# An empty scheduling step moved from the end of a tile to its middle, in two generators of a hybrid-encoder kernel

## The chip, the cores and the metric

The kernel runs on one core of one Trainium2 chip. The metric is the device time of one execution in microseconds (us). The engines are TensorE (PE; its weight loads are listed as PEld), VectorE (DVE), ScalarE (ACT), GpSimd (POOL), and SyncE (SP), whose queue issues the transfers. Each engine works through its own list of instructions in order, and the engines wait for each other by semaphores.

## The reference: what is computed

One encoder layer is applied to 1280 rows, of which 1024 are one request and 256 another, each row 2048 wide. The rows are normalised and multiplied by one wide weight matrix. Its columns feed three mixers, whose outputs are gated, joined and multiplied by an output matrix.

```python
hn = rms_norm(x, norm_g)
proj = hn @ w_in
xbc, z_ssd, dt_raw, q, k, v, z_att, mq, z_mem = split_cols(proj, IN_SIZES)
...
y_f = ssd_scan(xs, dt[:, :, 0], A[0], Bm, Cm)
y_b = ssd_scan(xs[:, ::-1], dt[:, ::-1, 1], A[1], Bm[:, ::-1], Cm[:, ::-1])[:, ::-1]
...
o_att = window_attention(q, k, v, sink) * jax.nn.silu(z_att)
...
sm = jnp.einsum('bthd,bmhd->bhtm', mq, mk).astype(jnp.float32) * (MEM_HEAD_DIM ** -0.5)
pm = jax.nn.softmax(sm, axis=-1).astype(mv.dtype)
o_mem = jnp.einsum('bhtm,bmhd->bthd', pm, mv).reshape(b, T, MEM_WIDTH) * jax.nn.silu(z_mem)

return x + jnp.concatenate([o_ssd, o_att, o_mem], axis=-1) @ w_out
```

The scan runs in chunks of 128 rows. From each chunk come a state product (B transposed times the weighted inputs) for either direction and a product inside the chunk, the diagonal part. Memory attention has four heads of 128 over 256 memory rows.

## The kernel before, in words

The rows are ten tiles of 128, eight of the long request (0 to 7) and two of the short one (8 and 9). The weight matrices go by in blocks of columns. Each block is a loop over the depth of the product: a weight tile is loaded (`wraw`, four buffers), ACT rounds it to its high part (`wh`, line 206), DVE takes the rest (`wl`, line 207; three buffers each), and PE multiplies both parts with the rows' two parts into PSUM tiles called `acc` (lines 258 to 260 and 293 to 295). A step of that loop is 15 matmuls of 512 columns (288 in the block `kv`) or 24 of 320 columns.

The mixers run beside these blocks. Each is a Python generator per tile: `attn`, `mem_attn`, `ssd_up` (the ascending pass of the scan), `ssd_down` and some preparations. Two queues of generators, the lanes, take turns. After each step of a block, `pump` adds the lane's rate to a credit and runs one generator step for each whole credit: the code up to the next `yield`. A step that has nothing between two `yield`s is empty: it uses up a credit and leaves time to what was issued before it. A generator that reaches its end is taken off its lane in that step, and the next one starts with the next credit. So the place of a piece of work in a generator sets beside which block matmuls it lands; a scheduler then orders the instructions of neighbouring steps a little further, with the work of the weight split ahead of the rest.

In memory attention a tile goes through these pieces: `scores(0)` and `scores(1)` (two heads each: products `pms`, maxima, exponentials and division into `mpr`), `turn_(0)` and `turn_(1)` (PE transposes, `pmt<-identr,mprw` at line 631; ACT copies them to `mpT`, line 819), `values(0)` and `values(1)` (PE products `pmo<-mpT,mv`, line 830, multiplied with the gate by DVE into `moT`) and the store. `fetch_next` loads the next tile's input ahead.

In `ssd_up` a tile begins with transposes `pxs` and the products `pcb`. Then for each of two head groups g come a product with the state (`pyf`, line 934), the weighted inputs for both directions, rounded by ACT (`fh`, line 931, and `bh`) with the rests by DVE (`fl`, `bl`), and two state products `pst` of three matmuls each (lines 917 to 919). At the end `diag` does the products inside the chunk, `py`, which ACT copies to `yo` and SP stores to `yd`.

All products beside the blocks share three PSUM tiles, the pool `mix`. Such a product waits until the tile it gets has been emptied by DVE or ACT.

Of the kernel before, what the change touches and what calls it, by code (L numbers as in the profile page):

```python
# [44 lines left out]
def hymba_encoder_kernel(  # L45
# [37 lines left out]
    def psum(name):  # L83
        return mix.tile([P, 512], F32, tag="mix", name=name)
# [37 lines left out]
    def rsqrt(dst, src, scale, n):  # L122
        G.tensor_scalar(out=dst, in0=src, scalar1=scale, scalar2=EPS, op0=ALU.mult, op1=ALU.add)
        G.tensor_tensor(out=dst, in0=dst, in1=mhalf[:, :n], op=ALU.pow)

    def hv(ap, n=8):
        return ap.rearrange("p (h d) -> p h d", h=n)

    def hb(ap, n, d):
        return ap.unsqueeze(2).broadcast_to([P, n, d])  # L130
# [287 lines left out]
    def w2(name):  # L418
        return mp.tile([P, 512], F32, tag="wa", name=name, bufs=WA)
# [86 lines left out]
    def taken(name, t):  # L506
        return fetched.pop((name, t)) if (name, t) in fetched else fetch[name](t)

    def fetch_next():

        name = lanes[0][1][0] if len(lanes[0]) > 1 else ("", 0)
        if name[0] in fetch:
            fetched[name] = fetch[name[0]](name[1])
# [109 lines left out]
    def slot(i, name, shape, dtype=F32):  # L623

        return mp.tile([P] + shape, dtype, tag=f"lg{i}", name=name, bufs=1)
# [3 lines left out]
    def turn_words(out, words, wrote):  # L629

        i = T.transpose(out.bitcast(F32R), words, identr)  # L631
        for w in wrote:
            tc.add_manual_dep(i.ins, w.ins.name, WRITTEN, reason="the words' writer")

    def as_words(i, name, shape):

        w = slot(i, name, shape, F32R)
        G.memset(w.bitcast(F32)[(slice(None),) + tuple(slice(n - 1, n) for n in shape)], 0.0)  # L638
        return w
# [115 lines left out]
    def mem_attn(t):  # L755
        grp, ti = divmod(t, 5)
        tc_ = slice(ti * P, (ti + 1) * P)
        qr = taken("mem_attn", t)
        q = qr.bitcast(F32)
        yield  # L760

        def turned():
            ps = psum("pmq")
            for h in range(4):
                T.transpose(ps[:, h * P:(h + 1) * P].bitcast(F32R), qr[:, h * P:(h + 1) * P], identr)
            return ps

        tok_ = turned() if grp == 0 else q
        sq = w2("sq")
        A.activation(sq, tok_, AF.Square)  # L770
        ss = sm.tile([P, 4], F32, tag="s4", name="mss", bufs=4)
        V.reduce_sum(out=ss, in_=hv(sq, 4), axis=AX.X)
        r = sm.tile([P, 4], F32, tag="s4", name="mr", bufs=4)
        rsqrt(r, ss, 1.0 / P, 4)
        yield
        feat_ = q if grp == 0 else turned()
        qh = mp.tile([P, 512], F32R, tag="qT", name="mqh", bufs=2)
        A.activation(qh, feat_, AF.Copy)
        ql = mp.tile([P, 512], F32R, tag="qT", name="mql", bufs=2)
        V.tensor_sub(ql, feat_, qh.bitcast(F32))  # L780
        z = w2("zm")
        S.dma_start(hv(z, 4), zT_d[1][grp][:, :, tc_])
        yield
        yield
        st_ = {}

        def scores(hp):
            ps = psum("pms")
            for j in range(2):
                h = 2 * hp + j  # L790
                c = slice(h * P, (h + 1) * P)
                o = ps[:, j * 256:(j + 1) * 256]
                T.matmul(o, qh[:, c], mkH[:, h, :], start=True, stop=False)
                T.matmul(o, qh[:, c], mkL[:, h, :], start=False, stop=False)
                T.matmul(o, ql[:, c], mkH[:, h, :], start=False, stop=True)
            m = sm.tile([P, 2], F32, tag="m2", name="mm", bufs=10)
            V.reduce_max(out=m, in_=hv(ps, 2), axis=AX.X)
            V.scalar_tensor_tensor(out=m, in0=m, scalar=-1.0, in1=r[:, 2 * hp:2 * hp + 2], op0=ALU.mult, op1=ALU.mult)
            pr = slot(hp, "mpr", [512])
            den = sm.tile([P, 2], F32, tag="m2", name="mden", bufs=10)  # L800
            for j in range(2):
                A.activation(pr[:, j * 256:(j + 1) * 256], ps[:, j * 256:(j + 1) * 256], AF.Exp,
                             scale=r[:, 2 * hp + j:2 * hp + j + 1], bias=m[:, j:j + 1], accum_out=den[:, j:j + 1])
            V.reciprocal(out=den, in_=den)
            wrote = []
            for j in range(2):
                c = slice(j * 256, (j + 1) * 256)
                wrote.append(V.tensor_scalar(out=pr[:, c], in0=pr[:, c], scalar1=den[:, j:j + 1], scalar2=0.5,
                                             op0=ALU.mult, op1=ALU.mult))
            st_[hp] = wrote  # L810

        def turn_(hp):
            wrote = st_[hp]
            pr = as_words(hp, "mprw", [513])
            pt = psum("pmt")
            for a in range(4):
                turn_words(pt[:, a * P:(a + 1) * P], pr[:, a * P:(a + 1) * P], wrote[a // 2:a // 2 + 1])
            pT = slot(hp, "mpT", [512])
            A.activation(pT, pt, AF.Copy)
            st_[hp] = pT  # L820

        oT = w2("moT")

        def values(hp):
            pT = st_.pop(hp)
            po = psum("pmo")
            for j in range(2):
                h = 2 * hp + j
                for a in range(2):
                    T.matmul(po[:, j * P:(j + 1) * P], mv[:, a, h * P:(h + 1) * P],  # L830
                             pT[:, (2 * j + a) * P:(2 * j + a + 1) * P], start=(a == 0), stop=(a == 1))
            c = slice(hp * 256, (hp + 1) * 256)
            V.tensor_mul(oT[:, c], po[:, :256], z[:, c])

        scores(0)
        yield
        scores(1)
        yield
        yield
        yield  # L840
        turn_(0)
        yield
        turn_(1)
        yield
        values(0)
        fetch_next()
        yield
        values(1)
        S.dma_start(oT_d[1][grp][:, :, tc_], hv(oT, 4))
        yield  # L850


    def wb(name, dtype=F32, shape=(P, 512)):
        return mp.tile(list(shape), dtype, tag="wb", name=name, bufs=WBB)

    def ssd_up(t):
# [65 lines left out]
        for g in range(2):  # L922
            c = slice(g * 512, (g + 1) * 512)
            a = mp.tile([P, 512], F32, tag=f"ya{g}", name="ya", bufs=1)
            ya.append(a)
            rows(g)
            if not last:
                xf = wb("xf")
                V.tensor_mul(hv(xf), hv(xsT[g]), hb(dd_all[:, (t + 1) % 6, 8 * g:8 * g + 8], 8, 64))
                fh = wb("fh", F32R)  # L930
                A.activation(fh, xf, AF.Copy)
            if not first:
                pf = psum("pyf")
                T.matmul(pf, bc[:, 2 + g, :], state[:, c], start=True, stop=True)
                V.tensor_mul(hv(a), hv(pf), hb(eacs_all[:, t, 8 * g:8 * g + 8], 8, 64))
            yield
            if not last:
                fl = wb("fl", F32R)
                V.tensor_sub(fl, xf, fh.bitcast(F32))
            if not first:  # L940
                xb = wb("xb")
                V.tensor_mul(hv(xb), hv(xsT[g]), hb(dd_all[:, (t + 1) % 6, 16 + 8 * g:24 + 8 * g], 8, 64))
                bh = wb("bh", F32R)
                A.activation(bh, xb, AF.Copy)
            yield
            if not last:
                ps = psum("pst")
                into(ps, g, fh, fl)
                if t == 0 and g == 0:

                    need(mk_prep, range(4))
                if first:
                    V.tensor_copy(state[:, c], ps)
                else:
                    V.tensor_mul(hv(state[:, c]), hv(state[:, c]), hb(cd_all[:, t, 8 * g:8 * g + 8], 8, 64))
                    V.tensor_add(state[:, c], state[:, c], ps)
                yield
            if not first:
                bl = wb("bl", F32R)
                V.tensor_sub(bl, xb, bh.bitcast(F32))  # L960
                yield
                ps = psum("pst")
                into(ps, g, bh, bl)
                st = wb("st")
                A.activation(st, ps, AF.Copy)
                S.dma_start(sb_d[t][:, c], st)
                yield
# [69 lines left out]
        yield  # L1037
        yield
        diag()
        yield  # L1040


    last_y = {}
# [740 lines left out]
```

## Time and profile before

| what | value |
|---|---|
| median of 3 runs | 1775.0 us (1774.94 to 1775.37) |
| the profiled execution's own time | 1773.26 us |
| its span, first to last instruction | 1771.5 us |
| PE busy | 1762.3 us (99%) |
| weight loads of PE busy | 1608.5 us (91%) |
| DVE, ACT, POOL busy | 1245.5, 918.9, 550.5 us |
| bytes moved by the transfers | 301.16 MB |
| granted TensorE clock, mean | 1.000 |

The profiled execution is 1.74 us below the median of the runs, and its span is 1.76 us shorter than its own time. Busy time of PE counts a matmul from its start to a modelled end, and matmuls overlap, so a row's length is more than the distance to the next start. How long PE stood still is therefore read from the starts of two rows that follow each other, compared with the distance of the same two kinds of instruction elsewhere.

### The profile page before, as it was taken

The numbers are of one execution on the slowest core, as the hardware profiler recorded it, in microseconds if no ns is written. First come the engines' busy times: TensorE is split into PE (matmuls) and PEld (weight loads), VectorE is DVE, ScalarE is ACT, GpSimd is POOL, SyncE is SP. The second block draws the span as 40 slices with busy tenths as digits, with TensorE's granted clock in tenths as the row PEclk, the third lists the DMA queues.
The fourth block names the chain that finished last, engine by engine and source line by source line (L and its number), as shares of the span: only waits on it lengthen the run. The fifth ranks groups of instructions, "written<-read, shape, count | busy, mean of one in ns | idle before, by whom it ended". The sixth has DMA issues, their size and how long they took to land. (4 is left out here: it accounts for less than half of the span.)

```text
span 1771.5 us, 32002 instructions
## 1 busy us (share of the span) xinstructions
PE 1762.3 (99%) x11046; PEld 1608.5 (91%) x11046; DVE 1245.5 (70%) x2348; ACT 918.9 (52%) x2049; POOL 550.5 (31%) x980
## 2 busy tenths in 40 slices
PE   9999999999999999999999999999999999999999
PEld 7889999999998999999889988888988888899999
DVE  5596788888858878778765676557777654766665
ACT  5555455555434766766464565544446633543332
POOL 0105789998810101011001000011110000058775
PEclk9999999999999999999999999999999999999999
DMA  8554444445347644454635654557777864644442
GB/s 301 193 184 122 140 151 146 145 141 170 121 138 214 185 145 138 143 162 115 188 120 179 196 154 155 170 164 252 223 245 232 255 189 147 219 142 149 144 144 77
DMA packets 208211, 301.16 MB, mean 170 GB/s; under 512 B 19569, under 2 KB 86193, under 8 KB 208049
## 3 DMA queue, kind: packets, MB, share of 16 engines
q1 hardware_dynamic: 207904, 299.06, 54.5%
q8 instruction: 87, 1.43, 0.3%
q14 instruction: 76, 0.61, 0.1%
q10 hardware_dynamic: 144, 0.06, 0.0%
HBM read 236.36 MB, written 62.69 MB: 169 GB/s over the span
## 5 line engine op out<-in xcount | busy, mean ns | idle before, releaser
L207 DVE TENSOR_TENSOR wl<-wraw,wh 128x512 fp32r<-128x512 f32 (+1 forms) x480 | 346.5, 724 | 236.9 <-ACT wh L206 226.2
L206 ACT ACTIVATE wh<-wraw 128x512 fp32r<-128x512 f32 (+1 forms) x480 | 292.2, 613 | 296.4 <-PE acc L260 153.3
L258 PE MATMUL acc<-wh,xH 128*128 128x512 f32 (+1 forms) x1088 | 418.2, 385 | 0.5 <-DVE v_all L337 0.4
L260 PE MATMUL acc<-wh,xL 128*128 128x512 f32 (+1 forms) x1088 | 410.2, 377 | 0.0
L259 PE MATMUL acc<-wl,xH 128*128 128x512 f32 (+1 forms) x1088 | 409.9, 377 | 0.0
L258 PEld LDWEIGHTS acc<-wh,xH 128*128 128x128 f32 x1088 | 204.2, 188 | 37.1 <-issue 2.7
L260 PEld LDWEIGHTS acc<-wh,xL 128*128 128x128 f32 x1088 | 204.2, 188 | 36.7 <-issue 0.2
L259 PEld LDWEIGHTS acc<-wl,xH 128*128 128x128 f32 x1088 | 204.4, 188 | 35.5 <-issue 1.2
L293 PE MATMUL acc<-xH,wh 128*128 128x320 f32 x640 | 202.9, 317 | 0.0
L206 ACT ACTIVATE sh<-ws 128x384 fp32r<-128x384 f32 x176 | 91.3, 523 | 208.3 <-POOL ws L1259 109.8
L294 PE MATMUL acc<-xL,wh 128*128 128x320 f32 x640 | 198.7, 310 | 0.0
L295 PE MATMUL acc<-xH,wl 128*128 128x320 f32 x640 | 198.4, 310 | 0.0
L207 DVE TENSOR_TENSOR sl<-ws,sh 128x384 fp32r<-128x384 f32 x176 | 124.4, 710 | 97.7 <-ACT sh L206 97.3
L1259 POOL TENSOR_TENSOR ws<-wraw 128x128 f32<-128x128 f32 x176 | 112.3, 638 | 208.2 <-DMA wraw<-in_w_in_pairs_dram 82.8
L293 PEld LDWEIGHTS acc<-xH,wh 128*128 128x128 f32 x640 | 120.1, 188 | 2.7 <-issue 2.1
L294 PEld LDWEIGHTS acc<-xL,wh 128*128 128x128 f32 x640 | 120.2, 188 | 1.5 <-issue 1.2
L295 PEld LDWEIGHTS acc<-xH,wl 128*128 128x128 f32 x640 | 120.2, 188 | 0.8 <-issue 0.7
L1259 POOL TENSOR_TENSOR ws<-wraw,ws 128x128 f32<-128x128 f32 x176 | 115.2, 654 | 13.8
L1259 POOL TENSOR_TENSOR wraw<-wraw 128x128 f32<-128x128 f32 x176 | 112.4, 639 | 13.7
L1259 POOL TENSOR_TENSOR ws<-ws,wraw 128x128 f32<-128x128 f32 x176 | 116.1, 659 | 0.0
L638 POOL MEMSET lgw<- 128x1 f32 x40 | 3.9, 99 | 311.3 <-DVE lg L701 187.3
L362 DVE SCALAR_TENSOR_TENSOR c<-u,vec,c 128x638 f32<-128x638 f32 (+1 forms) x96 | 90.1, 939 | 2.2 <-ACT c L357 1.6
(440 smaller groups left out, 3951.0 us busy)
## 6 DMA issues: line engine op xcount, KB each, us to landing
wraw<-in_w_in_laid_dram SPq DMA_DIRECT2D x176, 256.0 KB, 3.0
wraw<-in_w_in_pairs_dram SPq DMA_DIRECT2D x112, 256.0 KB, 2.7
wraw<-in_w_out_laid_dram SPq DMA_DIRECT2D x64, 256.0 KB, 3.5
wraw<-in_w_out_pairs_dram SPq DMA_DIRECT2D x64, 256.0 KB, 2.7
rf<-ac SPq DMA_DIRECT2D x40, 256.0 KB, 4.1
rb<-ac SPq DMA_DIRECT2D x40, 256.0 KB, 5.0
wraw<-in_w_mem_laid_dram SPq DMA_DIRECT2D x32, 256.0 KB, 4.2
xst<-in_x_sample_dram SPq DMA_DIRECT2D x20, 256.0 KB, 5.3
```

The lines of the kernel that those rows point to most:

```text
L206: a = A.activation(h, raw, AF.Copy)
L207: b = V.tensor_sub(l, raw, h.bitcast(F32))
L258: T.matmul(ps[t][:, :n], sh, h[:, :n], start=(k_ == 0), stop=False)
L259: T.matmul(ps[t][:, :n], sh, l[:, :n], start=False, stop=False)
L260: T.matmul(ps[t][:, :n], sl, h[:, :n], start=False, stop=(k_ == KT - 1))
L293: T.matmul(o, sh, cur["H", q][:, m, c], start=(k == 0), stop=False)
L294: T.matmul(o, sh, cur["L", q][:, m, c], start=False, stop=False)
L295: T.matmul(o, sl, cur["H", q][:, m, c], start=False, stop=(k == KT - 1))
L362: V.scalar_tensor_tensor(out=c[0], in0=u[:, k:k + n], scalar=cw[k], in1=c[0], op0=ALU.mult, op1=ALU.add)
L638: G.memset(w.bitcast(F32)[(slice(None),) + tuple(slice(n - 1, n) for n in shape)], 0.0)
L1259: G.tensor_tensor(out=o, in0=x, in1=y, op=op)
```

## The change

`mem_attn` has its fourth empty step ahead of `turn_(0)` instead of after `values(1)`. `fetch_next` stands one piece earlier in the code, in the same step counted from the tile's start as before. `ssd_up` has one more empty step ahead of the first state product of group 0, and none after `diag`. The number of steps per tile stays as it is in both, and so does everything that is computed.

```diff
         scores(0)
         yield
         scores(1)
-        yield
-        yield
-        yield
+        for _ in range(4):
+            yield
         turn_(0)
         yield
         turn_(1)
+        fetch_next()
         yield
         values(0)
-        fetch_next()
         yield
         values(1)
         S.dma_start(oT_d[1][grp][:, :, tc_], hv(oT, 4))
-        yield
...
                 bh = wb("bh", F32R)
                 A.activation(bh, xb, AF.Copy)
             yield
+            if g == 0:
+                yield
             if not last:
                 ps = psum("pst")
                 into(ps, g, fh, fl)
...
         yield
         yield
         diag()
-        yield
```

On PE, memory attention of tile 1 falls into the second pass of the block `kv` (288 columns). Before, the second turn stands five block matmuls and more behind the first, in two halves:

```order
L631 MATMUL pmt<-identr,mprw 128x128 x4
L258 MATMUL acc<-wh,xH_7440 128x288
L259 MATMUL acc<-wl,xH_7440 128x288
L260 MATMUL acc<-wh,xL_7441 128x288
L258 MATMUL acc<-wh,xH_7440 128x288
L631 MATMUL pmt<-identr,mprw 128x128 x2
L259 MATMUL acc<-wl,xH_7440 128x288
L631 MATMUL pmt<-identr,mprw 128x128 x2
```

In the changed kernel the second turn follows a whole step of 15 block matmuls later:

```order
L631 MATMUL pmt<-identr,mprw 128x128 x4
L258 MATMUL acc<-wh,xH_7428 128x288
L259 MATMUL acc<-wl,xH_7428 128x288
...
L260 MATMUL acc<-wh,xL_7429 128x288
L631 MATMUL pmt<-identr,mprw 128x128 x4
L258 MATMUL acc<-wh,xH_7428 128x288
```

The first turn keeps its place there, and the second moves behind eleven more block matmuls and comes in one piece.

On PE again, at a block's end in `ssd_up` of tile 1, before (`po` is the value product of window attention, `ppt` its transposes):

```order
L631 MATMUL ppt<-identr,lgw 128x128 x4
L934 MATMUL pyf<-state,bc 128x512
L293 MATMUL acc<-xH_6806,wh 128x320
L726 MATMUL po<-pT,v_all 64x128 x16
L917 MATMUL pst<-fh,bth 128x512
```

and in the changed kernel, where the lines of `ssd_up` are two lower (915 to 917, 932):

```order
L631 MATMUL ppt<-identr,lgw 128x128 x4
L915 MATMUL pst<-bh,bth 128x512
L916 MATMUL pst<-bl,bth 128x512
L917 MATMUL pst<-bh,btl 128x512
L932 MATMUL pyf<-state,bc 128x512
L726 MATMUL po<-pT,v_all 64x128 x16
L915 MATMUL pst<-fh,bth 128x512
```

The three matmuls of a state product of group 0 have come down by two steps of 24 block matmuls and stand between the transposes and the products that need them.

On ACT, memory attention of tile 8, in the output blocks, before:

```order
L206 ACTIVATE wh<-wraw 128x512
L819 ACTIVATE mpT<-pmt 128x512 x2
L206 ACTIVATE wh<-wraw 128x512
L770 ACTIVATE sq<-mq 128x512
L206 ACTIVATE wh<-wraw 128x512
```

and in the changed kernel:

```order
L206 ACTIVATE wh<-wraw 128x512 x2
L819 ACTIVATE mpT<-pmt 128x512
L206 ACTIVATE wh<-wraw 128x512
L819 ACTIVATE mpT<-pmt 128x512
L770 ACTIVATE sq<-mq 128x512
L206 ACTIVATE wh<-wraw 128x512 x2
```

A weight split now stands between the copies of the two turns. On PE at that place the second turn, before together with the first, comes a step later, straight ahead of both value products:

```order
L260 MATMUL acc<-wh,xL_16351 128x512
L631 MATMUL pmt<-identr,mprw 128x128 x4
L830 MATMUL pmo<-mpT,mv 128x128 x8
L258 MATMUL acc<-wh,xH_16350 128x512
```

No block matmul is left between them; before, a step of 15 stood there.

## The prediction

> **What bounds the kernel now.** I read the page first, then the waits of PE for the stretch in which the moved pieces run, then PE's timeline at each place that the two orders show moved. The page:
>
> ```profile
> span 1771.5 us, 32002 instructions
> PE 1762.3 (99%) x11046; PEld 1608.5 (91%) x11046; DVE 1245.5 (70%) x2348; ACT 918.9 (52%) x2049; POOL 550.5 (31%) x980
> PEclk9999999999999999999999999999999999999999
> ```
>
> PE is the bound from end to end, at full clock. Neither kernel has a matmul more or less than the other, so only PE's standstills can change the time. The waits of PE between 540 and 1480 us (who waited, for whom, total, times, longest):
>
> ```profile
> PE pst L917 <- ACT fh L931: 0.9, 1, 0.9
> PE pmt L631 <- DVE mpr L808: 0.6, 1, 0.6
> PE pr L631 <- ACT so L1063: 0.5, 1, 0.5
> PE pmo L830 <- ACT mpT L819: 0.2, 1, 0.2
> ```
>
> That is 2.2 us, and three of the four belong to moved pieces. Modelled ends swallow part of a standstill, so I go by starts: what is lost is the distance of two starts beyond what the first instruction needs elsewhere.
>
> A page of the Trainium skill speaks against so small a stake: Perfetto Trace Analysis, section Identifying the Most-Contended Engine, calls matmul busy time a poor measure of PE's distance from its limit and sends the reader to the busy share of the weight loads. By that rule 9% of the span would be open to gain.
>
> ```profile
> L258 PEld LDWEIGHTS acc<-wh,xH 128*128 128x128 f32 x1088 | 204.2, 188 | 37.1 <-issue 2.7 <-ACT kraw L334 0.6 <-ACT xH L200 0.5
> ```
>
> This row answers it: the loader idles 37.1 us on this line, almost all without a releaser, since a load takes 188 ns and a matmul of 512 columns starts every 0.23 us (1332.82 to 1333.05 below). I keep the rule as a rival with a small chance.
>
> **The change part by part.** A step moved by one place lands one step of the block later: 15 starts of 0.23 us, 3.4 us, in the blocks of 512 columns, and 15 of 0.13 us in `kv`. Of memory attention's 80 transposes 36 change their place among the block matmuls and of its 80 value products 48; the rest stay, because the scheduler sorts inside a step or because two steps fall behind the same block matmuls.
>
> *Second turn of memory tile 1, in `kv`.*
>
> ```profile
> 846.97 0.29 PE L260 MATMUL acc<-wh,xL 128*128 128x288 f32 x1
> 847.10 0.29 PE L258 MATMUL acc<-wh,xH 128*128 128x288 f32 x1
> 848.00 0.33 PE L631 MATMUL pmt<-identr,mprw 128*128 128x128 f32 x2 [0.60 <-DVE mpr L808]
> 848.17 0.38 PE L259 MATMUL acc<-wl,xH 128*128 128x288 f32 x1
> 848.38 0.29 PE L631 MATMUL pmt<-identr,mprw 128*128 128x128 f32 x2
> ```
>
> ```profile
> 847.50 0.62 DVE L808 TENSOR_SCALAR mpr<-mpr,mden 128x256 f32<-128x256 f32 x2
> ```
>
> A block matmul takes 0.13 us (846.97 to 847.10), so the turn was due at 847.23 and came at 848.00: 0.77 us lost, and 0.08 at the second half (848.17 to 848.38 is 0.21). DVE's division ends at 848.12. Eleven block matmuls later the turn is due about 1.4 us later than now: the wait goes. Gain **0.85**.
>
> *Value products of memory tiles 2 and 4, a state product of scan tile 1.*
>
> ```profile
> 849.90 1.05 PE L830 MATMUL pmo<-mpT,mv 128*128 128x128 f32 x8
> 850.71 0.38 PE L258 MATMUL acc<-wh,xH 128*128 128x288 f32 x1
> ```
>
> ```profile
> 876.81 1.06 PE L830 MATMUL pmo<-mpT,mv 128*128 128x128 f32 x8
> 878.10 1.16 PE L830 MATMUL pmo<-mpT,mv 128*128 128x128 f32 x8 [0.24 <-ACT mpT L819]
> ```
>
> ```profile
> 933.25 0.31 PE L294 MATMUL acc<-xL,wh 128*128 128x320 f32 x1
> 933.40 0.31 PE L295 MATMUL acc<-xH,wl 128*128 128x320 f32 x1
> 933.80 1.05 PE L830 MATMUL pmo<-mpT,mv 128*128 128x128 f32 x7
> ```
>
> ```profile
> 656.70 0.71 PE L293 MATMUL acc<-xH,wh 128*128 128x320 f32 x1
> 657.34 1.10 PE L726 MATMUL po<-pT,v_all 128*64 128x128 f32 x16
> ```
>
> A half of the values (x8) takes 0.81 us undisturbed. In tile 2 the next half starts 1.29 us on: 0.48 lost. The changed order puts the first half behind three block matmuls and the second behind twelve more: gain **0.48**. In tile 4 a start of 0.15 became 0.40; one more block matmul stands ahead: gain **0.15**. At 656.70 a 0.15 us start became 0.64 because `po` waits for its transposes' copies; the state product that now stands between (three starts of 0.23, less one block matmul of 0.15) covers the 0.49: gain **0.49**.
>
> *Second turn of memory tile 7.*
>
> ```profile
> 1387.77 0.46 PE L631 MATMUL pmt<-identr,mprw 128*128 128x128 f32 x4
> 1388.07 0.50 PE L910 MATMUL pxs<-identr,xc 128*128 128x128 f32 x4
> 1388.40 0.46 PE L258 MATMUL acc<-wh,xH 128*128 128x512 f32 x1
> 1388.82 0.54 PE L631 MATMUL pmt<-identr,mprw 128*128 128x128 f32 x4
> ```
>
> A start of 0.42 where 0.23 is due; fourteen block matmuls later it is gone: gain **0.19**.
>
> *First state product of scan tile 8,* the largest wait of the view and the one the extra step stands ahead of.
>
> ```profile
> 1332.82 0.39 PE L260 MATMUL acc<-wh,xL 128*128 128x512 f32 x1
> 1333.05 0.80 PE L631 MATMUL pmt<-identr,mprw 128*128 128x128 f32 x8
> 1334.72 0.50 PE L917 MATMUL pst<-fh,bth 128*128 128x512 f32 x1 [0.88 <-ACT fh L931]
> ```
>
> ```profile
> 1332.88 1.26 ACT L974 ACTIVATE rf<-rf,wj_all 128x128 f32<-128x128 f32 x4
> 1334.06 0.61 ACT L931 ACTIVATE fh<-xf 128x512 fp32r<-128x512 f32 x1
> ```
>
> Eight turns (0.30 for four, 1387.77 to 1388.07) end near 1333.65, so over 1.0 us is lost. The order shows the product only two block matmuls further, with four transposes gone from ahead of it, and ACT still has the four `rf` ahead of `fh`, which ends at 1334.67 as now. Two times 0.23 less 0.30: gain **0.1**; the rest, 0.9, stays.
>
> Gains: 0.85 + 0.48 + 0.15 + 0.49 + 0.19 + 0.1 = 2.3 us; at the least none, at the most 3.2 with the remaining 0.9.
>
> *New waits.* In memory tile 8 the second turn now stands ahead of both value products, with a weight split between the two copies on ACT.
>
> ```profile
> 1431.13 0.49 PE L830 MATMUL pmo<-mpT,mv 128*128 128x128 f32 x3
> ```
>
> ```profile
> 1431.38 0.63 ACT L206 ACTIVATE wh<-wraw 128x512 fp32r<-128x512 f32 x1 [2.53 <-issue]
> ```
>
> ```profile
> 848.76 0.60 ACT L819 ACTIVATE mpT<-pmt 128x512 f32<-128x512 f32 x1 [0.18 <-PE pmt L631]
> ```
>
> From the block's end, 1431.13, PE reaches the second value product after 0.30 + 0.81 = 1.1 us. ACT starts the split 0.25 us in, takes 0.63, then 0.60 for the copy: 1.5 us. Cost **0.4**; none if the copy finds ACT free, 1.0 if a second split gets ahead.
>
> Four places pile up products that share the three `mix` tiles: about 738 us (turns, `pyf`, scores of window attention, no block matmul between), 787 and 1382 us (`py` beside scores), 1389 us (`pxs` round a turn, then `pyf`). Their waits for emptying are not in the trace; the nearest row is one emptying by DVE that starts too late:
>
> ```profile
> 1389.45 0.69 DVE L912 COPY xs<-pxs 128x512 f32<-128x512 f32 x1
> ```
>
> So 0 to 0.7 each; since one or two other products cover most of each, I take 0.25: **1.0**. In sum new waits cost 1.4, between 0 and 3.8.
>
> *The transfers and POOL.* `fetch_next` keeps its step. The stores of `moT`, `sb`, `yp`, `yd` and the loads of `rf` and `rb` move with their steps past weight loads on SP, 1168 transfers in both. In the last scan tiles `diag` is now in the step just before `ssd_down` begins, which loads `yd` back. SP's waits between 1425 and 1470 us:
>
> ```profile
> SPq L213 <- DVE wl L207: 11.4, 6, 2.8
> ```
>
> Weight loads wait for a free buffer, up to four splits ahead of use; a store that holds the queue takes from that wait. The reader of `yd` is nine steps away. I cost both at nothing; without that cover, a late weight tile costs PE what it is late. On POOL one pair of small instructions swaps.
>
> Sum: -2.3 + 1.4 = -0.9. The profiled execution would go from 1773.26 to 1772.4; the runs' median lies 1.74 us above it, so **1774.1 us**.
>
> **The rivals.** *The piled products eat the gain*: new waits near their upper end, 3.8 - 2.3 = +1.5, 1776.5. For it: three `mix` tiles serve both lanes. Against: most moved pieces keep block matmuls between them.
>
> *ACT's queue turns against PE, slower.* A copy `mpT` at ACT's head waits for a turn that now comes a step later, with a weight split queued behind it; if the split is late by the 3.4 us step, PE stands for it. In the view of `pmt`:
>
> ```profile
> who waited for it (us, times):
>   ACT wh L206: 7.6, 3
> ```
>
> Splits have waited so already, without PE waiting for a split in that stretch, since they run ahead; that speaks against it. It decides from two full steps lost in the 20 copies: 2 x 3.4 - 2.3 = +4.5, 1779.5.
>
> *More was hidden than I count.* All of 3.2 goes without new waits, and standstills inside modelled matmuls, the weight loads' idle time among them, go too: from 0.4 more on it is faster by over 0.2%; 1771.2 or less. Against it: outside these places starts are even. The skill's rule stands behind this case.
>
> *The scheduler undoes the shift*: 1775.0. The orders speak against it.
>
> **How the numbers follow.** My forecast (net -2.3 to 0) has 0.62, piled products 0.17, ACT's queue 0.10, hidden gain 0.10, no shift 0.01. A difference of 0.2%, 3.55 us, is about what a measurement of this kernel tells from none: under 1771.45 is faster, over 1778.55 slower. So faster 0.10, same 0.62 + 0.17 + 0.01 = 0.80, slower 0.10. The costs' bounds give 1775.0 - 3.2 = 1771.8 and 1775.0 + 3.8 = 1778.8; eight in ten lie within 1771.6 to 1777.2.
>
> **What would show it.** Right: no wait of `pmt` for `mpr` in `kv`; even starts at `po` near 657 and `pmo` near 878; the wait of `pst` for `fh` near 1334 still there; a new wait of about 0.4 of `pmo` for `mpT` near 1432. Wrong: waits of PE for `wl` or `wh` between 820 and 1480, new ones at `pcb`, `pyf` or `psc` of more than 0.7, or PE starts in the blocks that have become closer.

## The result, and the profile after

The changed kernel takes 1777.04 us (median of 22 runs) and the kernel before 1774.97 us (22 runs beside them): a ratio of 1.0012, 95% interval 1.0007 to 1.0018. That is 2.1 us more, inside the 0.2% that counts as no change here, but clearly not less. The forecast was 0.9 us less. The profiled execution took 1775.66 us with a span of 1774.0 us, 2.4 us more than the one of before. In 15 of the 22 runs the mean granted clock was 1.000 and their median is 1776.47 us, while the runs of the kernel before at 1.000 in the three series of runs below have medians of 1773.89 to 1774.49 us, so the loss does not come from a lower clock.

The page after, its span and PE's row:

```profile
span 1774.0 us, 31995 instructions
PE 1763.1 (99%) x11046; PEld 1608.5 (91%) x11046; DVE 1247.0 (70%) x2348; ACT 920.5 (52%) x2049; POOL 552.9 (31%) x980
```

PE has the same 11046 matmuls. The waits of PE between 540 and 1480 us in the changed kernel (who waited, for whom, total, times, longest):

```profile
PE psc L692 <- DVE nm L694: 1.2, 1, 1.2
PE pxs L908 <- DMA xc<-xbc_d: 0.9, 2, 0.7
PE pst L915 <- ACT fh L929: 0.7, 1, 0.7
PE pr L631 <- ACT so L1062: 0.5, 1, 0.5
PE pk L539 <- DVE kh L533: 0.4, 1, 0.4
PE pxs L908 <- ACT mpr L802: 0.2, 1, 0.2
```

The two waits of memory attention (`pmt` for `mpr` 0.6, `pmo` for `mpT` 0.2) are gone. Three new ones stand in their place: scores of window attention (`psc`) for the maxima that DVE takes, the scan's input transposes (`pxs`) for their load, and the transposes of k (`pk`) for their rounding. The prediction had a wait of more than 0.7 us at `psc` among its signs of being wrong, and that sign came; but none of its terms has a price for any of the three suppliers.

The view shows only part of a standstill, so I compared starts. Where the two kernels have issued exactly the same matmuls beside the blocks, the time at which the same block matmul starts says how far one kernel is behind. This table gives what each profile lost (+) or won (-) against the first profile of before, stretch by stretch. Its other columns are the experiments below.

| stretch of before, us | changed | scan half alone | memory half alone | tile 8 back | three repairs | before, again |
|---|---|---|---|---|---|---|
| up to 567 (nothing moved) | +0.86 | +1.89 | +2.84 | +0.27 | +0.18 | -0.70 |
| 567 to 600 | +0.43 | +0.56 | -0.14 | +0.32 | -0.15 | -0.14 |
| 600 to 763 | -0.17 | -0.15 | +0.01 | -0.15 | -0.06 | 0.00 |
| 763 to 799 | **+1.06** | +0.98 | -0.01 | +0.73 | +0.10 | -0.03 |
| 799 to 839 | +0.31 | +0.31 | +0.23 | +0.32 | +0.29 | 0.00 |
| 839 to 860 | **-0.87** | +0.26 | -0.85 | -0.91 | -0.88 | -0.06 |
| 860 to 888 | -0.41 | -0.09 | -0.11 | -0.40 | +0.05 | -0.39 |
| 888 to 1114 | -0.04 | +0.07 | -0.07 | -0.02 | +0.06 | +0.04 |
| 1114 to 1241 | -0.09 | +0.21 | +1.14 | +0.08 | +0.27 | +0.06 |
| 1241 to 1351 | +0.30 | +0.54 | +1.24 | -0.05 | -0.14 | +0.16 |
| 1351 to 1385 | +0.14 | +0.75 | +0.08 | +0.08 | +0.08 | 0.00 |
| 1385 to 1416 | **+0.99** | +0.59 | -0.20 | -0.14 | -0.16 | -0.01 |
| 1416 to 1433 | +0.29 | +0.01 | +0.29 | +0.29 | +0.30 | +0.01 |
| 1433 to 1466 | -0.06 | -0.09 | +0.01 | -0.06 | -0.06 | 0.00 |

The last column is the unchanged kernel profiled a second time. It shows which differences are chance: 0.70 us before 567, 0.39 at 860 to 888, 0.16 at 1241 to 1351. What the changed kernel lost and that column lacks is at 567, 763, 799, 1385 and 1416; what it won is at 839. From 567 to 1466 us the changed column adds up to +1.9. Of the 2.84 us in the first row of the memory half, about 1.5 were lost between 152.8 and 156.2 us, where the granted clock of that profile was 0.50.

**At 1385 us: the scan's input load.** PE in the changed kernel (start, length, instruction, and in brackets the wait):

```profile
1381.68 1.97 PE L991 MATMUL py<-rb,xs 128*64 128x128 f32 x32
...
1388.94 0.39 PE L260 MATMUL acc<-wh,xL 128*128 128x512 f32 x1
1390.02 0.51 PE L908 MATMUL pxs<-identr,xc 128*128 128x128 f32 x4 [0.70 <-DMA xc<-xbc_d]
1390.37 0.51 PE L631 MATMUL pmt<-identr,mprw 128*128 128x128 f32 x4
1391.10 0.51 PE L908 MATMUL pxs<-identr,xc 128*128 128x128 f32 x4 [0.22 <-DMA xc<-xbc_d]
```

and SP's queue, before:

```profile
1375.21 1.19 SPq L996 DMA_DIRECT2D yd<-yo  x2
1376.45 0.50 SPq L866 DMA_DIRECT2D xc<-xbc_d  x1
...
1378.14 0.47 SPq L866 DMA_DIRECT2D xc<-xbc_d  x1
```

and after:

```profile
1383.52 1.13 SPq L996 DMA_DIRECT2D yd<-yo  x2
1384.70 1.24 SPq L864 DMA_DIRECT2D xc<-xbc_d  x2
```

In both orders the loads of tile 9's input `xc` stand behind the two stores of tile 8's diagonal products `py`. These products came at 1373.44 us before and come at 1381.68 now. A step here lies 30 block matmuls further on (two times 15, 6.9 us), not the 15 that I took for all places. The transposes that read the load did not move: they begin at 1388.94 plus 0.23. A load takes 5.2 to 5.8 us to land here, so what had 6.4 us or more to spare before now has none. By starts PE loses 0.85 us ahead of the first transposes (1.08 less 0.23) and 0.43 ahead of the second (0.73 less the 0.30 of four transposes).

**At 763 us: ACT's queue.** ACT after, around the exponential of the scan's last decay mask (`rb` of line 980):

```profile
769.90 0.63 ACT L980 ACTIVATE rb<-rb 128x512 f32<-128x512 f32 x1 [1.78 <-DVE u L387]
770.44 0.42 ACT L396 ACTIVATE u<-acc 128x320 f32<-128x320 f32 x1
...
772.12 0.61 ACT L206 ACTIVATE wh<-wraw 128x512 fp32r<-128x512 f32 x1
```

and DVE after:

```profile
767.30 0.69 DVE L1000 TENSOR_TENSOR sk<-xs,dco 128x512 f32<-128x512 f32 x1
...
768.51 0.69 DVE L1002 TENSOR_TENSOR ya<-ya,sk 128x512 f32<-128x512 f32 x1
769.11 0.76 DVE L979 COPY_PREDICATED rb<-upper,rf 128x512 f32<-128x512 uint32 x1
...
772.76 0.69 DVE L207 TENSOR_TENSOR wl<-wraw,wh 128x512 fp32r<-128x512 f32 x1 [2.75 <-ACT wh L206]
773.37 0.68 DVE L984 TENSOR_TENSOR rb<-rb,cb 128x512 f32<-128x512 f32 x1
...
775.38 2.74 DVE L362 SCALAR_TENSOR_TENSOR c<-u,vec,c 128x646 f32<-128x646 f32 x3
```

The exponential waits at ACT's head for the choice of the mask on DVE (line 979, done at 769.87; the bracket names a small fill of DVE that ends at the same moment). Behind it wait the copy of the block's result (`u`, line 396) and, after that, the weight split. Before, the choice ran at 765.70 and the copy at 767.17; the copy is 3.3 us later now, of which 1.0 is the lag of the whole kernel at this place. DVE then idles 2.75 us for the split, has a multiplication, a second split and four convolution taps to do, and reaches the maxima at 778.04. PE stands for them:

```profile
777.21 0.31 PE L293 MATMUL acc<-xH,wh 128*128 128x320 f32 x1
778.71 0.44 PE L692 MATMUL psc<-kT,qT 128*128 128x384 f32 x1 [1.19 <-DVE nm L694]
```

**At 567 us: a cover that walked away.** Before, three matmuls of a state product stood just ahead of `pk`; they are one step later now, and PE reaches the second half of `pk` before its operand:

```profile
576.50 0.39 PE L917 MATMUL pst<-fh,bth 128*128 128x512 f32 x1
...
577.19 0.46 PE L539 MATMUL pk<-identr,kh 128*128 128x128 f32 x4
```

after:

```profile
577.25 0.28 PE L539 MATMUL pk<-identr,kh 128*128 128x128 f32 x2
577.90 0.36 PE L539 MATMUL pk<-identr,kh 128*128 128x128 f32 x2 [0.37 <-DVE kh L533]
```

### The profile page after: what moved, and what is told of

Read it like the earlier page. It is cut to its first block, busy times and chain, and to the rows that moved or that the text cites. A ratio compares the mean times of both kernels' runs of the same rounds, so it can differ in the third digit from the quotient of the medians.

```text
span 1774.0 us, 31995 instructions
## 1 busy us (share of the span) xinstructions
PE 1763.1 (99%) x11046; PEld 1608.5 (91%) x11046; DVE 1247.0 (70%) x2348; ACT 920.5 (52%) x2049; POOL 552.9 (31%) x980
## 5 line engine op out<-in xcount | busy, mean ns | idle before, releaser
L260 PEld LDWEIGHTS acc<-wh,xL 128*128 128x128 f32 x1088 | 204.2, 188 | 37.1 <-issue 0.5
L258 PEld LDWEIGHTS acc<-wh,xH 128*128 128x128 f32 x1088 | 204.4, 188 | 36.2 <-issue 2.5
```

The source lines that it names most:

```text
L258: T.matmul(ps[t][:, :n], sh, h[:, :n], start=(k_ == 0), stop=False)
L260: T.matmul(ps[t][:, :n], sl, h[:, :n], start=False, stop=(k_ == KT - 1))
```

## The experiments

### Either half alone

My theory after the two traces: all three new waits come from the scan's half. First kernel: only memory attention's half.

```diff
 mem_attn: as in the changed kernel
 ssd_up:   as before
```

> Only memory attention's half of the change; the scan keeps its empty step behind the diagonal products. Theory (the loss comes from the scan's half, whose moved pieces make three suppliers late: the second transposes of k near 577 us, the scores of window attention near 777 us, the scan's own input load near 1389 us): none of these three waits, the division wait of the turns in kv gone (0.8 us), the value products near 878 us closer (0.5), one new wait near 1432 us (0.3): about 1.1 us under the kernel before, ratio 0.9994. Rival (memory attention's turns around the scan's transposes near 1389 us take the mix tiles from each other): this half alone keeps the wait at 1389 us and is 0.5 to 1.5 us above before, ratio 1.0003 to 1.0008.

Second kernel: only the scan's half.

```diff
 mem_attn: as before
 ssd_up:   as in the changed kernel
```

> Only the scan's half of the change; memory attention as before. Theory: all three waits stand (0.6 at 577, 1.3 at 777, 1.4 at 1389 us), and none of memory attention's gains: about 3.2 us above before, ratio 1.0018. Rival (the memory half is the loss): within 0.5 us of before, ratio 0.9997 to 1.0003, no wait of the scan's transposes for their load at 1389 us.

Measured: the memory half 1775.15 us (11 runs; before 1775.10 us, 27 runs), ratio 0.9997 (0.9988 to 1.0006). The scan half 1778.84 us (11 runs), ratio 1.0016 (1.0006 to 1.0025). The waits of the scan half alone:

```profile
PE pst L917 <- ACT fh L931: 1.3, 1, 1.3
PE psc L692 <- DVE nm L694: 1.1, 1, 1.1
PE pmt L631 <- DVE mpr L808: 0.8, 1, 0.8
PE pxs L910 <- DMA xc<-xbc_d: 0.6, 1, 0.6
PE pk L539 <- DVE kh L533: 0.5, 1, 0.5
...
```

All three new waits are there, and the division's wait in `kv` stays. In the memory half's column of the table none of the three is there, and the 0.85 us of `kv` is. The rival, that the memory half brings the loss near 1389 us, falls: that stretch is 0.20 us shorter with it. The gain that I expected of the memory half, 1.1 us, cannot be told from none in its times. Its profiled execution lost 2.84 us before anything moved (1.5 of it with the clock), and 1.14 and 1.24 in two stretches where other transfers landed late (below).

### Tile 8 has its empty step at the end again

```diff
-            if g == 0:
+            if g == 0 and t != 8:
                 yield
...
         diag()
+        if t == 8:
+            yield
```

> The changed kernel, but scan tile 8 has its empty step at the end again. Theory (the diagonal products of tile 8 fall behind the whole end of an output block, and the loads of tile 9's input stand behind their stores on SP): the diagonal products go back to about 1375 us, the input's loads to about 1377, and the transposes do not wait: 1.4 us less at 1389 us than in the changed kernel; the waits at 577 and 777 us stay. Rival (the turns of memory attention between the transposes are what is in the way): the 1.3 us ahead of the transposes stay.

Measured in one execution, 1773.15 us: the products `py` are back at 1373.58 us, the loads at 1376.59 and 1378.28, and `pxs` does not wait. The stretch 1385 to 1416 goes from +0.99 to -0.14, 1.1 us against 1.4 expected; the 763 stretch keeps +0.73 and the one at 567 +0.32. The turns of memory attention still stand between the two halves of `pxs`, so they are not the cause.

### The loads ahead of the stores

Same steps as in the changed kernel, only the order of two pairs on SP:

```diff
             for g in range(2):     # diag of tile 8
                 o = wb("yo")
                 A.activation(o, py[g], AF.Copy)
-                S.dma_start(yd_d[t]..., o)
...
             # tile 9, behind both loads of xc
+            S.dma_start(yd_d[8]..., o)   # twice
```

> The changed kernel, but the two stores of scan tile 8's diagonal part are issued behind the loads of tile 9's input instead of ahead of them; no step moves. Theory (on SP the loads stand behind stores that wait for the diagonal products): the loads are issued at about 1383.3 instead of 1384.7 us and land as much earlier, the transposes' wait near 1389 us shrinks from 1.4 to 0.2 us. Rival (the displacement by a step behind the end of the output block is enough by itself, the stores add nothing): loads where they are, the wait stays at 1.3 to 1.4 us.

One execution, 1781.7 us. The load's wait vanishes, as the theory said. But the stretch 1385 to 1416 got worse, from +0.99 to +3.41, which neither the theory nor the rival expected. SP, DVE and PE of this kernel:

```profile
1386.73 1.02 SPq L866 DMA_DIRECT2D xc<-xbc_d  x2
1387.85 0.92 SPq L870 DMA_DIRECT2D yd<-yo  x2
```

```profile
1393.72 0.43 DVE L888 TENSOR_TENSOR cd<-cb,identr 128x256 f32<-128x256 f32 x1 [1.69 <-DMA yd<-yo]
...
1394.92 0.68 DVE L915 COPY xs<-pxs 128x512 f32<-128x512 f32 x1
```

```profile
1392.41 0.46 PE L913 MATMUL pxs<-identr,xc 128*128 128x128 f32 x4
...
1395.66 1.74 PE L937 MATMUL pyf<-state,bc 128*128 128x512 f32 x2 [1.75 <-DVE xs L915]
```

`cd`, a small operation of tile 9, takes the buffer of `yo` in the ring of four that all of the scan's 512-wide tiles share. It has to wait until the store out of that buffer has landed, 5.8 us after its issue, and it stands at DVE's head with the emptying of `pxs` behind it. In the changed kernel the same operation already waited 0.15 us for that store. So the diagonal step of tile 8 carried two deadlines with it, the load behind its stores and the landing of its stores; putting one first makes the other late. What has to go back is the step.

Not all of the 3.41 us belongs to the order of the transfers. The view by stretches (window, its length, busy time of five engines, granted clock, busy share of the transfers, GB/s) shows half the clock just behind `pyf`:

```profile
1396.00:1399.40 3.40, 3.40 (x8) 2.06 (x7) 2.09 (x4) 0.59 (x1) 0.00 (x0) 0.50 0.64 212
```

From the start of `pyf` to the seventh block matmul behind it PE took 3.96 us here. In the first attempt at all repairs (below), which has the same edit and a granted clock of 1.00 there, the same matmuls took 2.35 us, and the stretch lost 2.06. So 1.6 of the 3.41 us went with the clock, and 1.8 to 2.1 us are the price of this order, still more than the 0.99 of the changed kernel. The time of 1781.7 us as a whole is no measure of the edit: a second stretch at half the clock, from 1338.0 to 1341.4 us, and a wait of 1.7 us for `fh` put 2.87 us into 1241 to 1351.

### The skip term behind the choice

The place at 763 us, with PE's order and DVE's amount of work unchanged:

```diff
         weights(2)
-        skip(1)
+        if t != 2:
+            skip(1)
         yield
         yield
         choose(3)
         yield
+        if t == 2:
+            skip(1)
```

> The changed kernel, but in scan tile 2 the skip term (two DVE operations of 0.69 us) comes behind the choice of the last mask instead of ahead of it; PE's order is the same and DVE has the same work. Theory (near 770 us ACT's queue is held by the exponential of the last decay mask, which waits for that choice on DVE; behind it stand the copies of the block's result and the weight split, and so the convolution's taps and the maxima of window attention come late): the exponential starts about 1.2 us earlier, the wait of PE for the maxima near 777 us shrinks from 1.3 to 0.2 us. Rival (DVE has more work ahead of the maxima, a multiplication and three taps, whatever ACT does): the wait stays at 1.0 to 1.4 us.

Measured: the exponential starts at 768.72 instead of 769.90 us, and the scores wait no more.

```profile
768.72 0.63 ACT L980 ACTIVATE rb<-rb 128x512 f32<-128x512 f32 x1 [1.14 <-DVE u L387]
```

```profile
776.85 0.61 DVE L694 CUSTOM_DVE_ANT_0 lg<-pdist,psc,nsink 128x384 f32<-128x384 bf16 x1
```

DVE reaches the maxima at 776.85 us, 1.2 us earlier, and the stretch goes from +1.06 to -0.07. DVE still has the multiplication, the split and the four taps ahead of the maxima; the rival falls. The one execution took 1776.19 us all the same, 0.5 more than the profile of the changed kernel: what it won here and at 567 (0.5) it lost where the edit does nothing (0.4 us ahead of 567, 0.5 at 860 to 888, 0.9 between 1114 and 1351, 0.3 at 1385 to 1416). The last of these is the load's wait again: the first transposes start 0.14 us behind its landing, as in the changed kernel (0.13), though the view of the waits puts the 1.2 us down to an operation of DVE that ended beside it.

### The repairs together

The first attempt combined the stores behind the loads, the skip term, and tile 0's step at the end.

> The changed kernel with both repairs (stores of tile 8 behind tile 9's loads, skip term of tile 2 behind the choice) and the empty step of scan tile 0 at the end as before. Theory: the three new waits go but for some tenths, 2.6 us under the changed kernel and 0.4 under before: ratio 0.9998 (0.9990 to 1.0003). Rival (what the waits cost comes back at the next supplier): 1.0008 or more, as the changed kernel.

1777.5 us (12 runs; before 1774.22 us, 17 runs), ratio 1.0022 (1.0014 to 1.0031): the rival's side, and the trace says why: +2.06 us at 1385 to 1416, where `pyf` again waited 1.7 us for DVE, and -0.08 at 763. In nine of its twelve runs the mean granted clock was below 1.000; the other three have a median of 1775.72 us against 1773.89 for the 13 such runs of before, so the loss at full clock is nearer 1.8 us than 3.3. An earlier kernel had put the step back at the end in the tiles 0, 2 and 8 (the edit of tile 8, for all three):

> The changed kernel, but scan tiles 0, 2 and 8 have their empty step at the end again (the three at which the trace shows the new waits). Theory: the three waits go (0.6, 1.3, 1.4 us), the gains stay: about 1.1 us under before, ratio 0.9994, 3.2 us under the changed kernel. Rival (any shift makes as many waits elsewhere): new waits of together 1 us or more at other places, ratio 1.0000 or above.

1774.66 us (11 runs), 0.9997 (0.9988 to 1.0006): no gain that can be told, but the loss is gone. Neither the wait at 777 nor that at 1389 us is in its trace. The last one has the step back in tiles 0 and 8, and the skip term moved in tile 2:

> The changed kernel with its empty step back at the end in scan tiles 0 and 8, and the skip term of scan tile 2 behind the choice of the last mask; tiles 1 and 3 to 7 keep the moved step. Theory (the loss comes from the displacement of tile 8's diagonal products and from ACT's queue in tile 2): no wait above 0.4 us at 777 and 1389 us; the gains of memory attention (0.9 in kv) against small losses of the scan's half (0.5): 0.3 us under before, ratio 0.9998 (0.9990 to 1.0005), and 2.4 under the changed kernel. Rival (each repair of this schedule brings a new wait, as moving the stores did): a new wait of more than 1 us in 540 to 1480 us, ratio 1.0010 or more.

1773.23 us (11 runs; before 1774.39 us, 27 runs), ratio 0.9995 (0.9986 to 1.0004). Its interval lies below that of the changed kernel (1.0007 to 1.0018) and holds 1. Its waits between 540 and 1480 us:

```profile
PE pr L631 <- ACT so L1067: 0.5, 1, 0.5
PE pmo L830 <- ACT mpT L819: 0.3, 1, 0.3
PE psc L692 <- DVE nm L694: 0.2, 1, 0.2
PE pst L915 <- ACT fh L929: 0.2, 1, 0.2
PE pxs L908 <- ACT mpr L802: 0.2, 1, 0.2
```

So the tiles 0, 2 and 8 hold the loss, and the moved step does no harm that can be told in the other scan tiles. That this kernel is faster than before is not shown.

### What is chance, and the wait that was left

> The kernel before once more, to tell chance from change: if the waits of the changed kernel near 577, 777 and 1389 us come from the change, none of them is here above 0.4 us; the wait of the state product near 1334 us, which was 0.3 to 1.9 us in the profiles so far, and single waits of about 1.2 us for transfers may differ from those of the first profile by up to 1 us.

It took 1772.16 us in its one execution. None of the three waits is there; the state product near 1334 us waited 1.0 us. Unexpected was the stretch 860 to 888, 0.39 us shorter than in the first profile though nothing differs: the value products of memory tile 2 came in one piece,

```profile
875.68 2.09 PE L830 MATMUL pmo<-mpT,mv 128*128 128x128 f32 x16
```

where the first profile had 1.29 us between two halves of eight. The 0.48 us that the prediction counted there was a feature of one execution.

Then I tried the largest wait that the change leaves, `pst` for `fh` near 1334 us, with and without memory attention's half (in all tiles but 8):

```diff
-        expo(0)
+        if t == 8:
+            with tc.issue_after(<the first fh>):
+                expo(0)
+        else:
+            expo(0)
```

> The kernel before with only the last edit of fh_mem: the four rf of scan tile 8 behind the first fh. Theory: only the wait near 1334 us goes, 0.9 us under before, ratio 0.9995 (0.9988 to 1.0002). Rival (the rf come late elsewhere): a new wait of the diagonal products or of the masks behind 1336 us, ratio 1.0000 or more.

> The kernel before with memory attention's half in all tiles but tile 8, no change of the scan's steps, and in scan tile 8 the four operations rf (1.26 us on ACT) behind the first rounding fh, which the largest wait of PE near 1334 us ends with. Theory: that wait shrinks from about 1.0 to 0.1 us, the division's wait in kv goes (0.9), no wait near 1432: 1.5 to 2 us under before, ratio 0.9990 (0.9983 to 0.9997). Rival (the input of the output blocks is what is late on ACT near 1330 us, a transfer by chance, and the rf only fill that time): the wait stays at 0.3 us or more, ratio 0.9995 or more.

1773.71 us, 0.9996 (0.9987 to 1.0005), and 1774.91 us, 1.0005 (0.9996 to 1.0013), 11 runs each. The wait stayed at 0.4 and 1.1 us although the four `rf` now stand behind `fh`: ACT's roundings of the output blocks' input, ahead of `fh`, wait for their transfers. With memory attention's half:

```profile
1330.37 0.83 ACT L200 ACTIVATE xH<-chd,vec 128x640 fp32r<-128x640 f32 x1 [0.51 <-DMA chd<-oT]
1331.88 0.83 ACT L200 ACTIVATE xH<-chd,vec 128x640 fp32r<-128x640 f32 x1 [0.68 <-DMA chd<-oT]
1332.62 0.61 ACT L931 ACTIVATE fh<-xf 128x512 fp32r<-128x512 f32 x1
```

This is the rival of the kernel with memory attention's half. The rival of the kernel without it, the four `rf` late elsewhere, shows in no wait of PE from 1337 to 1400 us, though 1351 to 1385 lost 0.37 us there (and 0.51 in the other kernel), and nothing here says why. Neither beats the kernel before by more than chance.

## Why the prediction was wrong

The size was inside the range (1771.6 to 1777.2) and inside "within 0.2%", which had 0.80; the direction was wrong. That the time lies inside is luck: the range reaches so far up for waits on the three `mix` tiles, and the rival of the piled products even gives 1776.5 us, but those waits did not come. Term by term:

- **The division's wait in `kv`, 0.85.** Right: 0.87 in the changed kernel, 0.85 to 0.91 in every kernel with the memory half, and not in the scan half alone.
- **Value products of tile 2, 0.48.** Wrong: 0.39 of it went away in the unchanged kernel too, and with the moved pieces the stretch goes from -0.41 to +0.05. One profile was taken for the kernel.
- **State product ahead of `po`, 0.49.** Wrong: the 0.64 us behind 656.70 does not go when the copies are early. In the changed kernel they end at 657.63 us, and `po` still starts only 0.83 us later, 0.52 behind the last matmul of `pyf` (0.67 before):

```profile
657.40 1.12 PE L932 MATMUL pyf<-state,bc 128*128 128x512 f32 x2
658.46 1.98 PE L726 MATMUL po<-pT,v_all 128*64 128x128 f32 x32
```

  The gap belongs to `pyf`: in all 16 places of the kernel before PE is held up behind its second matmul, whatever comes there (last section). The stretch 600 to 670 lost 0.08 us.
- **Tile 4, 0.15, and tile 7, 0.19.** Tile 4 is not found in the memory half alone (-0.05 in 888 to 951); tile 7 is (-0.20 in 1385 to 1416), but the load's wait came on top of it.
- **`pst` for `fh`, 0.1 of 1.0.** Right that the wait stays: 0.7 us in the changed kernel, 0.2 to 1.9 in the ten other profiles with the same ACT order. The wait is as long without the step (0.9 and 1.0 in the two profiles of before), so what it lost or won here is chance; the rows of ACT above point to a late transfer.
- **The new wait in memory tile 8, 0.4.** Right in place; 0.29 to 0.32 in every kernel that moves it, none in the others.
- **Four pile-ups of 0.25.** None to be seen: 670 to 763 us lost nothing, the skip term alone clears 763 to 799 down to -0.07, 1351 to 1385 lost 0.14, and with tile 8's step back 1385 to 1416 is 0.14 shorter than before.
- **"The transfers and POOL", costed at nothing.** This is the step that failed. I asked who waits behind `yd`'s stores and answered with the weight loads and with the reader of `yd`, nine steps away. I did not ask what else stands behind them on SP, the next tile's input, nor who needs the buffer that they empty. Price: 1.2 us (0.99 and the 0.20 that the memory half wins there). That the step is 15 block matmuls long everywhere was wrong at the same place: it was 30. (The count of transfers, 1168, is 1167 in both traces; nothing hangs on it.)
- **The rival "ACT's queue turns against PE"** had the right engine and the wrong instruction. I named the copy `mpT`; the one that held the queue was the scan's exponential, 1.06 us at 763. I had followed the moved pieces on PE and not the two engines that feed them: the extra step moves `choose`, `weights` and `skip` too.
- **Covers.** I credited a moved state product with covering `po`, and did not look where it had stood: ahead of `pk`, whose operand it covered. Price 0.3 to 0.6 us in four of the five profiles with that move and none in the fifth. It is not clear of chance: in the kernel with the step back in the tiles 0, 2 and 8 the stretch lost 0.40 as well, since DVE ran that much later against PE there, and the kernel that changes tile 8 alone (the four `rf` behind `fh`) lost 0.28. No experiment tests this cause by itself.

In sum, of 2.3 us of gains 1.0 came (`kv` and tile 7), of 1.4 us of new waits 0.3, and some 2.8 us of waits came that were not on the list (1.2, 1.06 and about 0.5). That is +2.1 us, against +1.9 by the table and 2.1 by the medians. What is left over, some tenths at 799 to 839 (0.31, with either half alone as well), is open: no experiment looked at it, and the won and lost tenths at 860 to 888 and 1241 to 1351 are within chance. The rule in the Trainium skill (Perfetto Trace Analysis, Identifying the Most-Contended Engine) that I kept as a rival gave no hint of this loss; the load row's idle time went from 37.1 to 36.2 us while the kernel became slower:

```profile
L258 PEld LDWEIGHTS acc<-wh,xH 128*128 128x128 f32 x1088 | 204.4, 188 | 36.2 <-issue 2.5
```

## What to carry to other kernels

When a step moves, list for every instruction in it, the stores above all, what stands behind it in the same queue and who needs the buffer that it frees; the loads of the next tile are the first to check. Look also at what the moved piece covered at its old place. And where a term of some tenths rests on one profile, take it as chance until a second execution of the same kernel shows it. Read the granted clock of a stretch before its length is put down to the change.

## What the runs showed of the hardware that I had not expected

Two executions of one kernel differ by single waits of about 1 us; those that I followed hang on the landing of one transfer. Twice (the memory half alone, and the step back in three tiles) a copy on ACT waited for the landing of an earlier store near 1227 us, and PE behind it:

```profile
1228.04 0.60 ACT L326 ACTIVATE qs<-acc 128x512 f32<-128x512 f32 x1 [1.36 <-DMA mq<-qs]
```

That cost 1.14 and 1.30 us in that stretch, while the other profiles lost 0.6 us or less there. The runs of the kernel before spread from 1772.49 to 1777.74 us, and such waits are a part of it.

The granted clock is another part. In the thirteen profiles it fell to 0.50 three times ahead of the last 2 us of the span, for 3.4 us each: at 152.8 us in the memory half alone, and at 1338.0 and 1396.0 us with the stores behind the loads. Block matmuls of 512 columns then start 0.43 us apart instead of 0.23, and each fall costs some 1.5 us. Each begins within 0.4 us of the end of a wait of PE of 1.7 to 1.9 us (the first in two parts, 2.2 us apart). Three other waits of that size have no fall behind them. In the kernel of the first attempt at all repairs, whose trace has such a wait, nine of twelve runs were below 1.000, and of the kernel before 14 of 71. That a long wait brings the fall, and so costs twice, fits this but is not shown.

The product `pyf`, whose operands the code does not mark as `fp32r`, holds PE up after it. Behind its last matmul the next one starts within 0.10 us, but the one after that only 0.39 to 0.64 us later, where 0.07 to 0.23 is usual. That is so in all 16 places of the kernel before, whatever follows.
